# Head of a decoder layer on one core: low parts moved from GpSimd to VectorE, value projections ahead of the compression, block additions in single steps

## The chip, the cores and the metric

The kernel runs on one core of one Trainium2 chip. The metric is device time in microseconds (us) of one execution. Engines are named as in the profile: PE (TensorE matmul), PEld (its weight load), DVE (VectorE), ACT (ScalarE), POOL (GpSimd), SP (SyncE, which here issues the weight loads).

## The reference, cut to what matters

One decoder layer over 512 positions of width 1024, all in float32. What the change touches is the part in front of the attention:

```python
n = rmsnorm(h, g_mix[l])
proj = n @ w_in[l]
(b_gate, c_gate, h_conv, q, k_c, v_c, k_s, v_s, k_w, v_w, g_br, ...) = jnp.split(proj, ...)
k_cmp = compress(kvh(k_c), cmp_pos_k[l], cmp_w1_k[l], cmp_w2_k[l], n_cmp)
v_cmp = compress(kvh(v_c), cmp_pos_v[l], cmp_w1_v[l], cmp_w2_v[l], n_cmp)
o_all = nsa_attention(q, k_cmp, v_cmp, selb(k_s), selb(v_s), winp(k_w), winp(v_w), ...)

def compress(kv, pos, w1, w2, n_cmp):
    blk = kv[:, idx] + pos[None, None, :, None, :]      # 31 blocks of 32 positions, step 16
    return jax.nn.gelu(blk @ w1) @ w2
```

Attention with 16 heads over 4 key and value heads follows (compressed, selected and window branch), then a gated merge with a short convolution, an output projection and a SwiGLU feed-forward block with two RMS norms.

## The kernel before, in words

Every product is made from three matmuls (`mm`, lines 117 to 121): each float32 operand is split into a high part in the matmul type (fp32r) and a low part, the rest, and high by high, high by low and low by high are added in PSUM. So each weight chunk costs, besides its load, one ACT copy that makes the high part `wh` (line 95) and one subtraction that makes the low part `wl` (line 96). `split` (lines 92 to 103) takes the engine of the subtraction as an argument; without one it is GpSimd. The pool `wp` has three buffers each of `raw`, `wh` and `wl`: the load of a chunk waits until the split of the third chunk before it is done, and `wh` waits until PE has used up the third chunk before it.

The order of PE's instructions is the order of the program; the order on the other engines is set by a scheduler at build time, from the program's order, priorities and its own estimate of times. [...]

The head, in the order of PE before the change:

- Lines 187 to 202: eight chunks `wc` (512 columns) with the loads of x. Per chunk ACT makes `nH` and `wh`, DVE makes `nL` (line 192), POOL makes `wl` (DVE for the first chunk alone), PE runs 12 matmuls into four PSUM banks `pc`. This is the projection from which the compressed keys and values are made.
- Lines 210 to 232: `rstd` (its power on POOL, line 211), four small transposes on PE, their copy `rstdb`, and four multiplications that evacuate `pc` into `kcs`, on DVE.
- Line 430, `build_blocks(0)` (lines 235 to 255): eight DVE additions of 64x496 (line 247) and then one ACT copy and one DVE subtraction over 128x2048, which make `bh` and `bl`, the operands of the key compression. `blk`, `bh` and `bl` have one buffer each.
- Line 431: two key projections (`wk`, 1024 columns, 24 matmuls each), evacuated by `k_post` (lines 395 to 412): one DVE multiplication, four ACT copies into `KH`, two DVE subtractions (line 410) and two DVE copies (line 411) into `KL`.
- Lines 432 to 434: four times a quarter of the first value projection (`v_proj(0, q)`, `wv`, 560 columns, 24 matmuls, low part on POOL) followed by a quarter of the key compression (`hidden(0, bk, q)`, `w1`, 1024 columns, 12 matmuls, low part on POOL). The last quarter of `v_proj` is followed by its evacuation (lines 336 to 346, ACT and DVE in turn, eight small instructions each).
- Line 435, `build_blocks(1)`; line 437, `gelu` of the key compression at a raised priority; line 438, the first query projection (`wq`, low part on DVE); lines 439 to 446 the second value projection (low parts on DVE) in turn with the value compression (low parts on POOL), with the transposes of gelu and the small product `k_cmp` between; line 448 the second `gelu`; line 449 one more key projection (`wk[1]`, low part on DVE).
- From line 713 on: attention. `score(0, 0)` (line 476) is its first matmul; the remaining projections are fed between its steps by `Fill`, and their low parts stay on POOL. `gelu_T(gv)` needs the second gelu and stands behind `score(0, 0)`, four steps of the query projection `wq[1]` and `score(0, 1)`.

Of the kernel before, what the change touches and what calls it, by code (L numbers as in the profile page):

```python
# [9 lines left out]
AF = mybir.ActivationFunctionType  # L10
ALU = mybir.AluOpType
# [20 lines left out]
def f(ap):  # L32
    return ap.bitcast(F32)
# [18 lines left out]
def trace(tc, a):  # L52
    nc = tc.nc
# [38 lines left out]
    def split(raw, n, eng=None):  # L92
        h = wp.tile([P, 1024], F32R, name="wh")
        l = wp.tile([P, 1024], F32R, name="wl")
        nc.scalar.activation(h[:, :n], raw[:, :n], AF.Copy)  # L95
        ins = (eng or nc.gpsimd).tensor_tensor(l[:, :n], raw[:, :n], f(h[:, :n]),  # L96
                                               op=ALU.subtract)
        if eng is None and scaled:

            tc.add_manual_dep(ins.ins if hasattr(ins, "ins") else ins, scaled[-1],  # L100
                              mybir.DependencyInfo(mybir.DependencyClass.Sync,
                                                   mybir.DependencyReason.SCHED_ONLY))
        return h, l

    def wchunk(src, n=1024, eng=None):
        return split(load(src, n), n, eng)
# [80 lines left out]
    for k in range(KD):  # L187
        xT = ep.tile([P, S], F32, name="xT", bufs=4)
        nc.sync.dma_start(xT, a["xT"][k])
        raw = load(a["wc"][k], 512)  # L190
        nc.scalar.activation(nH[:, k], xT, AF.Copy, scale=gmix[:, k:k + 1])
        nc.vector.scalar_tensor_tensor(nL[:, k], in0=xT, scalar=gmix[:, k:k + 1],
                                       in1=f(nH[:, k]), op0=ALU.mult, op1=ALU.subtract)
        wh, wl = split(raw, 512, nc.vector if k == 0 else None)
        for m in range(4):
            c = slice(m * P, (m + 1) * P)
            mm(pc[m], (wh[:, c], wl[:, c]), (nH[:, k], nL[:, k]), k == 0, k == KD - 1)
        if 3 <= k < 3 + NT:
            t = k - 3
            xt = ep.tile([P, D], F32, name="xt", bufs=2)  # L200
            nc.sync.dma_start(xt, a["x"][t])
            nc.scalar.activation(xt, xt, AF.Square, accum_out=ss[:, t:t + 1])
# [29 lines left out]
    kcs = kcs[1:] + kcs[:1]  # L232


    def build_blocks(v):
        blk = ep.tile([P, L2, KVH, NB], F32, name="blk")
        nc.gpsimd.memset(blk[:, :, :, NB - 1:NB], 0.0)
        for ct in range(2):
            kc = kcs[2 * v + ct]
            for hp in range(2):  # L240
                rows = slice(hp * HD, (hp + 1) * HD)
                for lp in range(2):
                    s0 = kc[rows, lp:lp + 1]
                    src = bass.AP(tensor=s0.tensor, offset=s0.offset,
                                  ap=[s0.ap[0], [2, L2], [16, NB - 1]])
                    pos = posd[v][rows, lp, :].unsqueeze(2).to_broadcast([HD, L2, NB - 1])
                    nc.vector.tensor_tensor(  # L247
                        blk[lp * HD:(lp + 1) * HD, :, 2 * ct + hp, 0:NB - 1],
                        src, pos, op=ALU.add)
        bh = ep.tile([P, L2, KVH * NB], F32R, name="bh")  # L250
        bl = ep.tile([P, L2, KVH * NB], F32R, name="bl")
        bv = blk.rearrange("p l h n -> p l (h n)")
        nc.scalar.activation(bh, bv, AF.Copy)
        nc.vector.tensor_tensor(bl, bv, f(bh), op=ALU.subtract)
        return bh, bl

    hid = {}

    def hidden(v, b, q):
        if q == 0:  # L260
            hid[v] = tp_tile()[:, 0:256]
        wh, wl = wchunk(a["w1"][v, q])
        for l in range(4):
            l2 = 4 * q + l
            c = slice(l * 256, (l + 1) * 256)
            mm(hid[v], (b[0][:, l2], b[1][:, l2]), (wh[:, c], wl[:, c]), l2 == 0, l2 == L2 - 1)
# [23 lines left out]
    def k_cmp(gT, w):  # L290
        ps = tp_tile()
        o = ps[:, 0:P]
        for c in range(2):
            cc = slice(c * P, (c + 1) * P)
            mm(o, (w[0][:, cc], w[1][:, cc]), (gT[0][:, cc], gT[1][:, cc]), c == 0, c == 1)
        ov = o.rearrange("p (g n) -> p g n", n=NB)
        for ct in range(2):
            oc = ov[:, 2 * ct:2 * ct + 2]
            nc.scalar.activation(KH[ct][:, :, 0:NB], oc, AF.Copy, scale=0.5)
            nc.vector.scalar_tensor_tensor(KL[ct][:, :, 0:NB], in0=oc, scalar=0.5,  # L300
                                           in1=f(KH[ct][:, :, 0:NB]), op0=ALU.mult,
                                           op1=ALU.subtract)
# [18 lines left out]
    def v_proj(br, kh):  # L321
        if kh == 0:
            sct, avt = sc_tile(), av_tile()
            vps[br] = [sct[:, 0:280], sct[:, S:S + 280], sct[:, 2 * S:2 * S + 280], avt[:, 0:280]]
        ps = vps[br]
        wh, wl = wchunk(a["wv"][br, kh], 560, nc.vector if br else None)
        for t in range(NT):
            for kk in range(2):
                k = 2 * kh + kk
                c = slice(kk * 280, (kk + 1) * 280)  # L330
                ts_ = slice(t * P, (t + 1) * P)
                mm(ps[t], (nH[:, k, ts_], nL[:, k, ts_]), (wh[:, c], wl[:, c]),
                   k == 0, k == KD - 1)
        if kh < 3:
            return
        for t in range(NT):
            src = ps[t][:, 0:256].rearrange("p (g d) -> p g d", d=HD)
            r = rstd[:, t:t + 1]
            nc.scalar.activation(VT[:, t, br, :, 0:HD], src, AF.Copy, scale=r)
            nc.vector.scalar_tensor_tensor(VT[:, t, br, :, HD:P], in0=src, scalar=r,  # L340
                                           in1=f(VT[:, t, br, :, 0:HD]), op0=ALU.mult,
                                           op1=ALU.subtract)
            gt = gates[:, t, br * 24:(br + 1) * 24]

            nc.scalar.activation(gt, ps[t][:, 256:280], AF.Exp, scale=nrs[:, t:t + 1])
            nc.vector.tensor_scalar_add(gt, gt, 1.0)
# [48 lines left out]
    def k_post(br, ct):  # L395
        def post(ps):
            kf = oyp.tile([P, S], F32, name="z")
            nc.vector.tensor_tensor(kf, ps, rstdb, op=ALU.mult)
            for hp in range(2):
                me = slice(hp * HD, (hp + 1) * HD)  # L400
                ot = slice((1 - hp) * HD, (2 - hp) * HD)

                def dst(t, rows):
                    return t[ct][rows, hp, NB:KC].rearrange("p (j b c) -> p b j c",
                                                            b=2, c=P)[:, br]

                src = kf[me].rearrange("p (j c) -> p j c", c=P)
                nc.scalar.activation(dst(KH, me), src, AF.Copy)
                nc.scalar.activation(dst(KH, ot), src, AF.Copy)
                nc.vector.tensor_tensor(dst(KL, me), src, f(dst(KH, me)), op=ALU.subtract)  # L410
                nc.vector.tensor_copy(dst(KL, ot), f(dst(KL, me)))
        return post
# [3 lines left out]
    def q_post(pr):  # L416
        def post(ps):
            q = oyp.tile([P, 2, S], F32R, name="q", bufs=2)
            lo, hi = slice(0, HD), slice(HD, P)
            nc.scalar.activation(q[lo, 0], ps[lo], AF.Copy)  # L420
            nc.scalar.activation(q[hi, 1], ps[hi], AF.Copy)
            nc.vector.tensor_tensor(q[hi, 0], ps[lo], f(q[lo, 0]), op=ALU.subtract)
            nc.vector.tensor_tensor(q[lo, 1], ps[hi], f(q[hi, 1]), op=ALU.subtract)
            Q[pr] = q
        return post

    def run(*jobs):
        Fill(jobs).finish()

    bk = build_blocks(0)  # L430
    run(Job(a["wk"][0], k_post(0, 0)), Job(a["wk"][2], k_post(1, 0)))
    for q in range(4):
        v_proj(0, q)
        hidden(0, bk, q)
    bv = build_blocks(1)
    with tc.high_priority(PRI2):
        gk = gelu(hid[0])
    run(Job(a["wq"][0], q_post(0), eng=nc.vector))
    v_proj(1, 0)
    gkT = gelu_T(gk)  # L440
    hidden(1, bv, 0)
    for q in range(1, 4):
        v_proj(1, q)
        if q == 1:
            k_cmp(gkT, w2k)
        hidden(1, bv, q)
    with tc.high_priority(PRI2):
        gv = gelu(hid[1])
    run(Job(a["wk"][1], k_post(0, 1), eng=nc.vector))


    units = [(pr, i) for pr in range(8) for i in range(NT)]
# [604 lines left out]
```

## Time and profile before

| what | us |
|---|---|
| runs of the kernel | 924.97, 927.70, 2294.02; median 927.7 |
| the profiled execution | 930.89 |
| its span, first to last instruction | 929.1 |
| PE busy | 905.9 |
| DVE busy | 521.7 |
| ACT busy | 425.9 |
| POOL busy | 161.3 |
| mean granted TensorE clock, of full | 0.987 |

[...]

### The profile page before, as it was taken

To read this page: it belongs to the slowest core of one execution; us is meant where nothing else is said; L and a number is where in the kernel's file an instruction comes from. 1 tells how busy PE (TensorE), PEld (TensorE's weight loads), DVE (VectorE), ACT (ScalarE), POOL (GpSimd) and SP (SyncE) were. 2 spreads that over 40 slices of the span, in tenths; PEclk is the share of its full clock that TensorE was granted. 3 is DMA by queue.
4 is the path that set the end of the run, shared out by engine and by line. 5 is a ranking of instruction groups with operands and counts; after the bars stand their busy time and mean duration, and the time that the engine had idled before them with its cause. 6 is when DMAs were issued, how large, how long until landed. Compare 5 with 4: busy or idle time off the path is not lost.

```text
span 929.1 us, 12775 instructions
## 1 busy us (share of the span) xinstructions
PE 905.9 (98%) x4757; PEld 766.4 (82%) x4757; DVE 521.7 (56%) x1194; ACT 425.9 (46%) x934; POOL 161.3 (17%) x100
## 2 busy tenths in 40 slices
PE   9878999999999999999999999999999999999996
PEld 7677888888888888878888999888888888888885
DVE  3698688888888788774555552333333333222223
ACT  6254676767667677673433532322332232212222
POOL 5543433232332322222000300000000000000200
PEclk9888999999999999999999999999999999999999
DMA  8323521211212121212622620223323332333212
GB/s 300 103 88 107 170 69 46 69 46 51 64 46 69 46 69 46 69 46 79 239 91 91 202 72 1 91 91 103 102 91 93 109 94 90 92 96 103 96 46 91
DMA packets 26271, 85.15 MB, mean 92 GB/s; under 512 B 3424, under 2 KB 3680, under 8 KB 26208
## 3 DMA queue, kind: packets, MB, share of 16 engines
q1 hardware_dynamic: 24912, 82.78, 27.9%
q10 hardware_dynamic: 1296, 1.55, 0.6%
q8 instruction: 37, 0.61, 0.3%
q14 instruction: 26, 0.21, 0.1%
HBM read 82.23 MB, written 2.10 MB: 91 GB/s over the span
## 4 chain that ended last, share of the span: by engine, by line
PE 89%; DVE 6%; DMA 2%; ACT 1%; issue 1%; POOL 1%; SPq 0%; POOLq 0%; ACTq 0%
PE acc L121 24%; PE acc L119 24%; PE acc L120 24%; PE sc L476 4%; PE tp L543 4%; PE av L561 2%; PE av L562 2%; DVE blk L247 2%; PE av L556 1%; DMA w2kr<-w2k 1%; DVE KL L410 1%; PE sc L120 1%; DMA xt<-x 0%; DMA xT<-xT 0%; PE sc L121 0%
## 5 line engine op out<-in xcount | busy, mean ns | idle before, releaser
L95 ACT ACTIVATE wh<-raw 128x1024 fp32r<-128x1024 f32 (+2 forms) x143 | 144.4, 1012 | 324.2 <-PE acc L120 123.5
L119 PE MATMUL acc<-nH,wh 128*128 128x512 f32 x656 | 263.7, 402 | 0.0
L121 PE MATMUL acc<-nH,wl 128*128 128x512 f32 x656 | 257.7, 393 | 3.4 <-DVE wl L96 3.4
L120 PE MATMUL acc<-nL,wh 128*128 128x512 f32 x656 | 257.2, 392 | 0.0
L96 DVE TENSOR_TENSOR wl<-raw,wh 128x1024 fp32r<-128x1024 f32 (+2 forms) x86 | 106.2, 1235 | 165.7 <-ACT wh L95 165.3
L96 POOL TENSOR_TENSOR wl<-raw,wh 128x1024 fp32r<-128x1024 f32 (+2 forms) x57 | 128.3, 2255 | 241.9 <-DVE pt L519 96.0
L121 PEld LDWEIGHTS acc<-nH,wl 128*128 128x128 f32 x656 | 123.9, 189 | 30.3 <-DVE wl L96 3.9
L120 PEld LDWEIGHTS acc<-nL,wh 128*128 128x128 f32 x656 | 124.3, 189 | 21.8
L119 PEld LDWEIGHTS acc<-nH,wh 128*128 128x128 f32 x656 | 124.3, 189 | 21.7
L121 PE MATMUL acc<-wh,aL 128*128 128x512 f32 (+1 forms) x198 | 73.4, 371 | 0.0
L119 PE MATMUL acc<-wh,aH 128*128 128x512 f32 (+1 forms) x198 | 73.4, 371 | 0.0
L120 PE MATMUL acc<-wl,aH 128*128 128x512 f32 (+1 forms) x198 | 73.4, 370 | 0.0
L503 ACT ACTIVATE pt<-pt,nm 128x128 f32<-128x128 f32 (+3 forms) x128 | 70.7, 554 | 2.4 <-DVE nm L488 1.8
L488 DVE CUSTOM_DVE_ANT_0 pt<-sc,tri,nrs 128x128 f32<-128x128 f32 (+3 forms) x128 | 65.4, 546 | 0.1
L547 DVE TENSOR_TENSOR tl<-tp,th 128x512 fp32r<-128x512 f32 x80 | 55.2, 690 | 13.0 <-ACT th L546 11.2
L894 DVE TENSOR_TENSOR sg<-acc,sg 128x512 f32<-128x512 f32 x22 | 15.2, 692 | 80.7 <-PE acc L121 80.7
L940 POOL TENSOR_TENSOR h<-h,gfin 128x512 f32<-128x512 f32 x4 | 6.0, 1546 | 299.1 <-ACT jk L922 299.1
L546 ACT ACTIVATE th<-tp 128x512 fp32r<-128x512 f32 x80 | 47.4, 593 | 13.0 <-PE tp L543 12.1
L543 PE MATMUL tp<-ident,pt 128*128 128x128 f32 x320 | 49.7, 277 | 0.1
L120 PEld LDWEIGHTS acc<-wl,aH 128*128 128x128 f32 x198 | 37.3, 188 | 7.1
L119 PEld LDWEIGHTS acc<-wh,aH 128*128 128x128 f32 x198 | 37.3, 188 | 7.1
L121 PEld LDWEIGHTS acc<-wh,aL 128*128 128x128 f32 x198 | 37.3, 188 | 7.0
(229 smaller groups left out, 1527.8 us busy)
## 6 DMA issues: line engine op xcount, KB each, us to landing
raw<-wg SPq DMA_DIRECT2D x22, 512.0 KB, 3.5
raw<-wu SPq DMA_DIRECT2D x22, 512.0 KB, 3.5
raw<-wd SPq DMA_DIRECT2D x22, 512.0 KB, 3.5
raw<-wcv SPq DMA_DIRECT2D x12, 512.0 KB, 3.5
raw<-w SPq DMA_DIRECT2D x8, 512.0 KB, 3.5
raw<-wq SPq DMA_DIRECT2D x8, 512.0 KB, 3.5
raw<-wgc SPq DMA_DIRECT2D x8, 512.0 KB, 3.5
raw<-wga SPq DMA_DIRECT2D x8, 512.0 KB, 3.5
```

What stands on the lines that cost most here:

```text
L95: nc.scalar.activation(h[:, :n], raw[:, :n], AF.Copy)
L96: ins = (eng or nc.gpsimd).tensor_tensor(l[:, :n], raw[:, :n], f(h[:, :n]), op=ALU.subtract)
L119: nc.tensor.matmul(ps, lhs[0], rhs[0], start=first, stop=False)
L120: nc.tensor.matmul(ps, lhs[0], rhs[1], start=False, stop=False)
L121: nc.tensor.matmul(ps, lhs[1], rhs[0], start=False, stop=last)
L247: nc.vector.tensor_tensor(blk[lp * HD:(lp + 1) * HD, :, 2 * ct + hp, 0:NB - 1], src, pos, op=ALU.add)
L476: nc.tensor.matmul(o, q[:, h, qs], kk[g // 2][:, g % 2, c0:c0 + n], start=(j == 0), stop=(j == 1))
L488: nc.vector.tensor_tensor_reduce(out=pt[:, r0:r0 + w].rearrange("p (j c) -> p j c", c=P), in0=sv[:, b], in1=tri[:, NT - 1 - i:NT], scale=n ...
L503: nc.scalar.activation(s, s, AF.Exp, scale=-1.0, bias=nm[:, b:b + 1], accum_out=U[u]["sm"][:, h, b:b + 1])
L543: nc.tensor.transpose(tp[:, (2 * b + h) * P:(2 * b + h + 1) * P], pts[h][:, r0:r0 + P], ident)
L546: nc.scalar.activation(th, tp, AF.Copy)
L547: nc.vector.tensor_tensor(tl, tp, f(th), op=ALU.subtract)
```

## The change

`split` of all eight `wc` chunks goes to DVE, and so do those of `w1` (in `hidden`), of both `wv`, of `wk[0]` and `wk[2]`; GpSimd makes no low part before attention starts. `build_blocks` becomes a generator that is stepped by hand (`build(n)`): each of its eight additions is one step, and the ACT copy and DVE subtraction are cut into two halves of 128x1024, one step each. In PE's order both value projections now stand ahead of all of the compression: `wk[0]`, `wk[2]`, the first value projection, `wq[0]`, the second value projection, four quarters of `hidden(0)`, `wk[1]`, four quarters of `hidden(1)` with `k_cmp` in their middle. `wk[1]` no longer stands between the last quarter of `hidden(1)` and `score(0, 0)`. The number of matmuls, loads and splits is as before.

```diff
--- before.py
+++ after.py
@@ -191,7 +191,7 @@
         nc.scalar.activation(nH[:, k], xT, AF.Copy, scale=gmix[:, k:k + 1])
         nc.vector.scalar_tensor_tensor(nL[:, k], in0=xT, scalar=gmix[:, k:k + 1],
                                        in1=f(nH[:, k]), op0=ALU.mult, op1=ALU.subtract)
-        wh, wl = split(raw, 512, nc.vector if k == 0 else None)
+        wh, wl = split(raw, 512, nc.vector)
         for m in range(4):
             c = slice(m * P, (m + 1) * P)
             mm(pc[m], (wh[:, c], wl[:, c]), (nH[:, k], nL[:, k]), k == 0, k == KD - 1)
@@ -231,6 +231,8 @@
         kcs.append(kc)
     kcs = kcs[1:] + kcs[:1]
 
+
+    blocks = {}
 
     def build_blocks(v):
         blk = ep.tile([P, L2, KVH, NB], F32, name="blk")
@@ -247,19 +249,22 @@
                     nc.vector.tensor_tensor(
                         blk[lp * HD:(lp + 1) * HD, :, 2 * ct + hp, 0:NB - 1],
                         src, pos, op=ALU.add)
+                    yield
         bh = ep.tile([P, L2, KVH * NB], F32R, name="bh")
         bl = ep.tile([P, L2, KVH * NB], F32R, name="bl")
         bv = blk.rearrange("p l h n -> p l (h n)")
-        nc.scalar.activation(bh, bv, AF.Copy)
-        nc.vector.tensor_tensor(bl, bv, f(bh), op=ALU.subtract)
-        return bh, bl
+        for c in (slice(0, 8), slice(8, 16)):
+            nc.scalar.activation(bh[:, c], bv[:, c], AF.Copy)
+            nc.vector.tensor_tensor(bl[:, c], bv[:, c], f(bh[:, c]), op=ALU.subtract)
+            yield
+        blocks[v] = bh, bl
 
     hid = {}
 
     def hidden(v, b, q):
         if q == 0:
             hid[v] = tp_tile()[:, 0:256]
-        wh, wl = wchunk(a["w1"][v, q])
+        wh, wl = wchunk(a["w1"][v, q], eng=nc.vector)
         for l in range(4):
             l2 = 4 * q + l
             c = slice(l * 256, (l + 1) * 256)
@@ -323,7 +328,7 @@
             sct, avt = sc_tile(), av_tile()
             vps[br] = [sct[:, 0:280], sct[:, S:S + 280], sct[:, 2 * S:2 * S + 280], avt[:, 0:280]]
         ps = vps[br]
-        wh, wl = wchunk(a["wv"][br, kh], 560, nc.vector if br else None)
+        wh, wl = wchunk(a["wv"][br, kh], 560, nc.vector)
         for t in range(NT):
             for kk in range(2):
                 k = 2 * kh + kk
@@ -427,26 +432,42 @@
     def run(*jobs):
         Fill(jobs).finish()
 
-    bk = build_blocks(0)
-    run(Job(a["wk"][0], k_post(0, 0)), Job(a["wk"][2], k_post(1, 0)))
+
+    V = nc.vector
+
+    def build(n):
+        for _ in range(n):
+            next(bg, None)
+
+    bg = build_blocks(0)
+    run(Job(a["wk"][0], k_post(0, 0), eng=V))
+    build(3)
+    run(Job(a["wk"][2], k_post(1, 0), eng=V))
+    build(3)
+    v_proj(0, 0)
+    build(2)
+    for q in range(1, 4):
+        v_proj(0, q)
+        build(1)
+    bg = build_blocks(1)
+    run(Job(a["wq"][0], q_post(0), eng=V))
     for q in range(4):
-        v_proj(0, q)
-        hidden(0, bk, q)
-    bv = build_blocks(1)
+        v_proj(1, q)
+        build(2)
+    for q in range(4):
+        hidden(0, blocks[0], q)
     with tc.high_priority(PRI2):
         gk = gelu(hid[0])
-    run(Job(a["wq"][0], q_post(0), eng=nc.vector))
-    v_proj(1, 0)
+    build(3)
+    run(Job(a["wk"][1], k_post(0, 1), eng=V))
     gkT = gelu_T(gk)
-    hidden(1, bv, 0)
-    for q in range(1, 4):
-        v_proj(1, q)
-        if q == 1:
-            k_cmp(gkT, w2k)
-        hidden(1, bv, q)
+    hidden(1, blocks[1], 0)
+    hidden(1, blocks[1], 1)
+    k_cmp(gkT, w2k)
+    hidden(1, blocks[1], 2)
+    hidden(1, blocks[1], 3)
     with tc.high_priority(PRI2):
         gv = gelu(hid[1])
-    run(Job(a["wk"][1], k_post(0, 1), eng=nc.vector))
 
 
     units = [(pr, i) for pr in range(8) for i in range(NT)]
```

## Rows read from the trace of the kernel before

**Rows 1.** The page's first part: busy time, share of the span, instructions.
```profile
PE 905.9 (98%) x4757; PEld 766.4 (82%) x4757; DVE 521.7 (56%) x1194; ACT 425.9 (46%) x934; POOL 161.3 (17%) x100
```

**Rows 2.** Waits of PE before 112 us: us in total, times, longest.
```profile
PE sc L120 <- DVE nL L192: 3.5, 1, 3.5
PE acc L121 <- DVE wl L96: 3.4, 1, 3.4
...
PE tp L121 <- DVE bl L254: 1.8, 1, 1.8
PE sc L476 <- ACT gates L345: 1.4, 1, 1.4
PE tp L119 <- ACT bh L253: 1.3, 1, 1.3
PE sc L120 <- POOL wl L96: 1.2, 1, 1.2
```

**Rows 3.** Windows: PE, PEld, DVE, ACT, POOL busy; granted clock, DMA share, GB/s.
```profile
29.40:35.00 5.60, 5.56 (x15) 4.40 (x16) 0.00 (x0) 0.67 (x1) 2.31 (x2) 0.50 0.47 145
...
53.00:59.00 6.00, 6.00 (x26) 5.85 (x27) 5.88 (x6) 1.64 (x4) 4.30 (x3) 0.51 0.30 92
...
76.90:82.90 6.00, 6.00 (x14) 4.75 (x15) 4.79 (x11) 5.41 (x11) 0.17 (x1) 0.51 0.44 135
...
110.70:118.00 7.30, 7.30 (x39) 6.35 (x40) 6.16 (x27) 6.13 (x19) 0.00 (x0) 1.00 0.22 67
30.00:110.70 80.70, 70.88 (x407) 63.48 (x405) 63.20 (x66) 34.10 (x56) 33.95 (x16) 0.88 0.37 117
...
200.00:400.00 200.00, 199.96 (x1118) 166.32 (x1117) 166.03 (x569) 141.92 (x405) 56.49 (x28) 1.00 0.18 56
```

**Rows 4.** DVE by tile: count, shortest/median/longest ns, first and last start.
```profile
L247 DVE TENSOR_TENSOR blk<-xT,posk x8: 994/1012/3004, 38.4 to 47.6; 64x496 f32<-64x496 f32 x8
...
L410 DVE TENSOR_TENSOR KL<-z,KH x6: 679/686/2765, 52.8 to 113.5; 64x512 fp32r<-64x512 f32 x6
L411 DVE CAST KL<-KL x6: 421/1471/2487, 54.2 to 114.6; 64x512 fp32r<-64x512 f32 x6
...
L346 DVE TENSOR_SCALAR gates<-gates x8: 161/175/2362, 77.6 to 110.8; 128x24 f32<-128x24 f32 x8
```

**Rows 5.** Timeline of DVE (first three) and POOL: start us, duration us, instruction.
```profile
20.73 0.75 DVE L192 SCALAR_TENSOR_TENSOR nL<-xT,gmix,nH 128x512 fp32r<-128x512 f32 x1 [2.33 <-ACT nH L191]
...
25.28 1.24 DVE L217 TENSOR_SCALAR nrs<-rstd 128x4 f32<-128x4 f32 x1 [1.14 <-POOL rstd L211]
...
26.51 2.88 DVE L192 SCALAR_TENSOR_TENSOR nL<-xT,gmix,nH 128x512 fp32r<-128x512 f32 x1
...
25.22 6.40 POOL L96 TENSOR_TENSOR wl<-raw,wh 128x512 fp32r<-128x512 f32 x3
```

**Rows 6.** PE timeline: first matmuls of v_proj(1, 3), hidden(1, 3), wk[1]; last of wk[1].
```profile
99.18 0.29 PE L119 MATMUL sc<-wh,nH 128*128 128x280 f32 x1
...
102.30 0.28 PE L119 MATMUL tp<-wh,bh 128*128 128x256 f32 x1
...
103.67 0.40 PE L119 MATMUL acc<-nH,wh 128*128 128x512 f32 x1
...
108.91 0.39 PE L121 MATMUL acc<-nH,wl 128*128 128x512 f32 x1
```

**Rows 7.** Timeline of DVE: two low parts.
```profile
75.59 1.23 DVE L96 TENSOR_TENSOR wl<-raw,wh 128x1024 fp32r<-128x1024 f32 x1
...
85.77 0.73 DVE L96 TENSOR_TENSOR wl<-raw,wh 128x560 fp32r<-128x560 f32 x1
```

**Rows 8.** DVE groups by form before 112 us: count, busy us, mean ns, idle.
```profile
L411 DVE CAST KL<-KL 64x512 fp32r<-64x512 f32 x4 | 7.9, 1978 | 0.1
...
L346 DVE TENSOR_SCALAR gates<-gates 128x24 f32<-128x24 f32 x8 | 5.4, 679 | 0.0
```

**Rows 9.** DMA issues before 112 us: KB each, median us from issue to landing.
```profile
raw<-w SPq DMA_DIRECT2D x8, 512.0 KB, 3.5
```

## Prediction, made before the changed kernel was built or run

> **What bounds the kernel now.** I read the page first: PE has work in flight for 905.9 of 929.1 us [rows 1], so only two things can be won without touching the matmuls: the time in which PE waits, and the time in which it runs at half its clock. The list of PE's waits then puts nearly all of the waiting into the head: six waits before 112 us, 12.6 us together [rows 2]. The reader is to see who ends them: four end with a DVE or POOL instruction, and the other two with an ACT instruction that stands behind DVE in the code (`bh` copies what the additions write, the gates come after `VT`). [...] Head and clock together lose 21.4 us, 2.3% of the kernel. Attention behind it has none to give: 199.96 of 200 us are busy between 200 and 400 us [rows 3].
>
> Why DVE is late is seen in its instructions. The same form takes 1.01 or 3.00 us (block additions), 0.42 or up to 2.49 (copies into `KL`), 0.16 or up to 2.36 (128x24 for the gates) [rows 4]. In the timeline the long ones lie under POOL's low parts: three of these occupy POOL for 6.40 us from 25.22, and in that time the product over 128x4 (line 217) takes 1.24 us and `nL` 2.88, where the `nL` before it took 0.75 [rows 5]. That `nL` ends at 29.39, and PE's wait of 3.5 us ends with it.
>
> **The change part by part.** The matmuls are the same, so PE's own time stays, and the sum is one of waits and clock, made against the profiled execution (930.9 us, span 929.1), which is 3.2 above the median of the runs shown, 927.7.
>
> *Removed, the waits.* If nothing replaced them, `score(0, 0)` would start at 110.7 - 21.4 = 89.3 us. A check from PE's own pace: a value quarter takes 3.12 us, a compression quarter 1.37, a key or query projection 5.47 (5.24 to its last matmul and that one's 0.23) [rows 6]. From the end of `wc`, four projections, eight value quarters, eight compression quarters and 0.8 us (estimate) of small products are 21.9 + 25.0 + 11.0 + 0.8 = 58.7 us.
>
> *The front.* Seven low parts of 512 columns go to DVE, each about 0.7 us by `nL` of the same width (0.75) [rows 5]. With eight `nL` they make 11 us of DVE work in a front of 20, so six are free. For the last chunk I keep the order of the queue (the two small products, which wait for the power on POOL, ahead of `nL`). With POOL free, the first takes about 0.17 instead of 1.24 (as the shortest of the gates [rows 4]), the second likewise, so `nL` runs from 25.6 to 26.3 and its low part to 27.0. PE wanted them at 25.9 (29.4 less its wait) and 0.2 later: a wait of 1.0 us in two pieces, instead of 3.5. Bounds: 0 if the queue puts `nL` first, 3.5 if nothing gets shorter. The low parts of `wk[0]` and `wk[2]`, 1.23 each [rows 7], follow until 29.5, where DVE had nothing to do (0.00 busy from 29.4 to 35.0 [rows 3]). PE finishes `wc` and the transposes at 25.9 + 1.0 + 2.9 = 29.8.
>
> *DVE between there and attention.* Now it is busy 63.2 us from 30.0 to 110.7 [rows 3]. Added: eight low parts of `w1` at 1.23 and four of `wv` at 0.73 [rows 7], 12.8 us. Removed: the lengthening, (1978 - 421) ns x 4 for the copies into `KL`, (679 - 161) ns x 8 for the gates, 2.0 us for one block addition [rows 4, 8], 12.3 us. So DVE has at most 63.7 us of work where PE has 58.7; other forms were longer too (one of line 410 took 2.77 instead of 0.68 [rows 4]), and I put the work at 58. **DVE is then as full as PE**, and its order decides how much waiting is left. Cutting `bh` and `bl` in halves adds nothing that counts.
>
> *First value projection.* All eight additions of the first `blk` and the evacuation of `wk[0]` stand ahead of its third low part. From 29.8: five evacuations of 512 columns at 0.7, eight additions at 1.01, `k_post` (0.7 + 2 x 0.68 + 2 x 0.42), two low parts at 0.73, half a `bl` at 1.2 and the low part itself sum to 17.9 us, so it ends at 47.7; with the second `k_post` ahead of it at 50.6. PE gets there after two projections and two quarters, at 47.0, and wants it 0.2 later. The wait is 0.5 to 3.4 us; I take 1.7, a little under the middle. After that DVE has the time of `wq[0]` and the second value projection, 18 us, for 8 additions, 7 low parts and the evacuation of the first `VT`, about 16, so it catches up. Both `wv` evacuations free the PSUM banks under `wq[0]` or under the compression; the 1.4 us for `gates` at `score(0, 0)` goes.
>
> *Compression in one piece.* From the end of `v_proj(1, 3)` to `score(0, 0)` PE needs 17.2 us (eight quarters, `wk[1]`, the small products). In this time DVE has seven low parts and two halves of `bl` at 1.23, 11.1 us, and some 4 of evacuation, gelu and `k_cmp` (estimate from their widths), none of which can begin earlier, since each low part waits for a buffer that PE frees three chunks before. I take 2.5 us of waits, between 0 (the work fits) and 5 (two low parts late by the 2.2 us of the evacuation). SP's queue: each quarter now needs 512 KB per 1.37 us; a load lands 3.5 us after its issue [rows 9], and the buffer for it is freed about two quarters and more ahead, so loads are hidden; uncovered, they would cost 3.5 - 2 x 1.37 = 0.8 us a quarter. POOL's queue loses the low parts and keeps `rstd`, so the power cannot come later than now.
>
> *Behind it.* The second gelu had 5.47 us of `wk[1]` as its cover; now it has `score(0, 0)`, four steps and `score(0, 1)`, about 3.8 us, for a chain of five instructions on two engines, and the low part of `wq[1]` is still POOL's and can lengthen one of them by 2. I take 1.0, between 0 and 3.
>
> *Clock.* The waits that halved it were 3.4 us or more, or two of 1.3 and 1.8 close together [rows 2, 3]; after the single 1.4 it stayed at 1.00 [rows 3]. One more stretch costs 2.9; I take 0.8, for a chance of about 0.3; bounds 0 and 5.8.
>
> Sum of what comes back: 1.0 + 1.7 + 2.5 + 1.0 + 0.8 = 7.0, so 14.4 us are saved; the check by PE's pace (29.8 + 58.7 + 1.7 + 2.5 + 0.8 = 93.5 instead of 110.7, less 1.0) gives 16.2. I take 15.5: 930.9 - 15.5 = 915.4, and less 3.2 for the median **912 us**. All bounds at the low end save 21.4 us by the waits and 23.2 by PE's pace (906 and 905), all at the high end 0.9 us (927).
>
> **The rivals.** *A, the queue fits.* Waits vanish but for the front: 20.4 us, 907. For it: the additions are single steps and DVE had idle time. Against: 58 us of work in 58.7.
>
> *B, one or two low parts come late by the length of a few additions*, as `wl` did before 76.9 us: each is 3.4 of wait and 2.9 of clock, 6.3; with one more than forecast 918, with two 925. For it: the order was laid out at build time on estimates, and DVE has no slack to mend it.
>
> *C, slower.* The long DVE instructions are not POOL's doing, or go to other waits, and DVE's queue sets the pace of the head: 12.8 us are added between 30 and 110.7 and nothing goes, 927.7 + 12.8 = 940.5. It decides from where less than 12.8 us of lengthening goes away and DVE's idle time stays. Against: the long ones begin and end with POOL's [rows 5].
>
> *D, many small waits hold the clock down.* Three more half-clock stretches of 2.9 us, 921. Against: 1.00 after the wait of 1.4 [rows 3]. [...]
>
> **How the numbers follow.** The forecast has 0.56, A 0.16, B 0.18, C 0.05, D 0.05. About 2% (18.6 us, to 909.1) is what a measurement of this kernel can tell from no change. Faster by more: all of A and a third of the forecast, 0.34. Slower by more (946): under half of C, 0.02. The rest, 0.64, is within. The range leaves out part of B, C and the lowest of A: 905 to 922; the forecast's own is 907 to 917.
>
> **What would show it.** In the profile after, `score(0, 0)` should start at 93 to 96 us; DVE's copies into `KL` at 0.42 and additions at 1.0; no wait of PE over 3 us; one wait for `nL` or `wl` of `wc` near 1 us; waits of 1 to 3 us on `wl` at the second or third value quarter and in the compression; POOL nearly idle from 26 us until `wq[1]`. The step on DVE's load is wrong if DVE is under 85% busy from 30 us to `score(0, 0)`; the whole is wrong if PE's waits there exceed 10 us, or if new waits appear in attention.

## The result and the profile after

The kernel after the change takes 919.18 us (median of 5 runs, 917.53 to 920.69), the kernel before in the same measurement 926.2 (median of four runs, 924.97 to 927.70). One more run of the kernel before, 2294.02 us, was disturbed and is left out here, while the 927.7 from which the forecast starts is a median that counts it. The ratio is 0.9922 with a 95% interval of 0.9899 to 0.9944: faster by some 7 us, inside the forecast range, but less than half of the 15.7 us that were forecast.

The profiled execution after is the fastest of its five, 917.53 us with a span of 915.7. The page's first part, after, against [rows 1]:

```profile
PE 898.8 (98%) x4757; PEld 760.2 (83%) x4757; DVE 515.5 (56%) x1217; ACT 426.3 (47%) x936; POOL 119.6 (13%) x79
```

PE's instructions are the same and its busy time is 7.1 us less: that is clock (8.8 us were lost to it before, half of the 17.6 us that [rows 3] show at 0.50 and 0.51; 1.7 are below). POOL lost 21 low parts and 41.7 us, DVE took them and is 6.2 us *less* busy. What PE waits for before 112 us, after (us in total, times, longest), against [rows 2]:

```profile
PE sc L119 <- ACT gates L350: 2.6, 1, 2.6
PE sc L120 <- DVE wl L96: 2.5, 1, 2.5
PE tp L184 <- DVE bh L181: 1.9, 1, 1.9
PE tp L120 <- DVE wl L96: 1.6, 2, 1.1
PE tp L119 <- ACT wh L95: 0.2, 1, 0.2
```

The third of these stands at the very start and is in every kernel here; the others make 6.9 us where there were 13.3 (the 12.6 of [rows 2], and 0.7 for one `wh` that the prediction's six waits leave out). No wait in the front is long enough for this list, but two matmuls of the last chunk start 0.52 and 0.60 us behind the one before them, where the pace is 0.23. So some 0.7 us are lost there in two pieces. PE's timeline after:

```profile
24.47 0.39 PE L119 MATMUL sc<-nH,wh 128*128 128x512 f32 x1
24.99 0.50 PE L120 MATMUL sc<-nL,wh 128*128 128x512 f32 x1
25.59 0.50 PE L121 MATMUL sc<-nH,wl 128*128 128x512 f32 x1
```

The windows after (columns as in [rows 3]):

```profile
29.40:35.00 5.60, 5.60 (x26) 4.65 (x25) 5.54 (x9) 0.67 (x1) 0.00 (x0) 1.00 0.38 102
...
45.20:50.00 4.80, 4.74 (x25) 4.74 (x26) 4.67 (x8) 3.81 (x6) 0.00 (x0) 0.64 0.35 109
...
64.30:70.00 5.70, 5.70 (x44) 5.70 (x45) 3.16 (x6) 2.23 (x4) 0.00 (x0) 1.00 0.39 126
...
30.00:97.20 67.20, 60.25 (x386) 54.99 (x386) 56.06 (x82) 34.91 (x58) 1.91 (x2) 0.97 0.39 120
200.00:400.00 200.00, 199.96 (x1123) 166.72 (x1123) 163.30 (x560) 140.23 (x398) 55.58 (x26) 1.00 0.17 54
```

One stretch of lowered clock is left, 0.64 over 4.8 us, which costs 0.36 x 4.8 = 1.7 us; there were three of some 6 us. Attention is as before. `score(0, 0)` starts at 97.21 instead of 110.70, 13.5 us earlier, and what follows it takes as long as before (818.5 and 818.4 us to the end of the span). So the whole difference between these two executions is in the head.

DVE by tile after (columns as in [rows 4]):

```profile
L249 DVE TENSOR_TENSOR blk<-xT,posk x8: 981/1010/1027, 32.9 to 42.9; 64x496 f32<-64x496 f32 x8
L249 DVE TENSOR_TENSOR blk<-xT,posv x8: 989/1010/1029, 51.0 to 62.3; 64x496 f32<-64x496 f32 x8
...
L415 DVE TENSOR_TENSOR KL<-z,KH x8: 674/685/690, 38.7 to 116.1; 64x512 fp32r<-64x512 f32 x8
L416 DVE CAST KL<-KL x8: 410/421/423, 40.3 to 117.0; 64x512 fp32r<-64x512 f32 x8
...
L351 DVE TENSOR_SCALAR gates<-gates x8: 166/168/177, 61.0 to 81.8; 128x24 f32<-128x24 f32 x8
```

The reader is to see the third number of each: the longest is now within 6% of the median, where it had been 3 to 15 times the shortest. In these groups the lengthening is gone.

Two waits remain that count. PE's timeline after:

```profile
45.26 0.40 PE L120 MATMUL sc<-wl,nH 128*128 128x280 f32 x1 [2.53 <-DVE wl L96]
...
61.30 0.39 PE L121 MATMUL acc<-nH,wl 128*128 128x512 f32 x1
64.28 0.39 PE L119 MATMUL sc<-wh,nH 128*128 128x280 f32 x1 [2.59 <-ACT gates L350]
```

The first is the second quarter of the first value projection. The second is the first matmul of the second value projection: it writes into the PSUM banks of the first, and waits until these are evacuated. DVE's timeline there, after:

```profile
57.00 2.03 DVE L249 TENSOR_TENSOR blk<-xT,posv 64x496 f32<-64x496 f32 x2
59.06 0.49 DVE L345 SCALAR_TENSOR_TENSOR VT<-sc,rstd,VT 128x256 fp32r<-128x256 f32 x1
59.58 1.01 DVE L249 TENSOR_TENSOR blk<-xT,posv 64x496 f32<-64x496 f32 x1
60.62 0.48 DVE L345 SCALAR_TENSOR_TENSOR VT<-av,rstd,VT 128x256 fp32r<-128x256 f32 x1
...
62.33 0.99 DVE L249 TENSOR_TENSOR blk<-xT,posv 64x496 f32<-64x496 f32 x1
63.35 0.18 DVE L351 TENSOR_SCALAR gates<-gates 128x24 f32<-128x24 f32 x1
63.43 0.48 DVE L345 SCALAR_TENSOR_TENSOR VT<-sc,rstd,VT 128x256 fp32r<-128x256 f32 x1
```

Additions of the *second* block (`posv`), which nobody needs until the value compression, stand ahead of and between the four `VT` that free the banks (the third `VT` is among the lines left out).

### The profile page after: what moved, and what is told of

Read it like the earlier page. It is cut to its first block, busy times and chain, and to the rows that moved or that the text cites. A ratio compares the mean times of both kernels' runs of the same rounds, so it can differ in the third digit from the quotient of the medians.

```text
span 915.7 us, 12776 instructions
## 1 busy us (share of the span) xinstructions
PE 898.8 (98%) x4757; PEld 760.2 (83%) x4757; DVE 515.5 (56%) x1217; ACT 426.3 (47%) x936; POOL 119.6 (13%) x79
## 4 chain that ended last, share of the span: by engine, by line
PE 88%; DVE 6%; DMA 2%; ACT 2%; issue 1%; SPq 0%; POOL 0%; POOLq 0%; ACTq 0%; DVEq 0%
PE acc L119 24%; PE acc L121 24%; PE acc L120 24%; PE sc L497 4%; PE tp L564 4%; PE av L582 2%; PE av L583 2%; DVE blk L249 2%; DVE wl L96 1%; PE av L577 1%; DMA w2kr<-w2k 1%; DMA raw<-wk 1%; ACT wh L95 1%; DMA xT<-xT 0%; DMA xt<-x 0%
## 5 line engine op out<-in xcount | busy, mean ns | idle before, releaser
L96 DVE TENSOR_TENSOR wl<-raw,wh 128x1024 fp32r<-128x1024 f32 (+2 forms) x107 | 123.4, 1154 | 170.1 <-ACT wh L95 170.0
L119 PEld LDWEIGHTS acc<-nH,wh 128*128 128x128 f32 x656 | 123.4, 188 | 21.4
L96 POOL TENSOR_TENSOR wl<-raw,wh 128x1024 fp32r<-128x1024 f32 x36 | 86.6, 2407 | 236.7 <-DVE pt L540 96.4
```

Source lines behind the costliest of these rows:

```text
L119: nc.tensor.matmul(ps, lhs[0], rhs[0], start=first, stop=False)
```

## The experiments

Ten runs follow: the two kernels once more, unchanged, and eight kernels with edits. Each computes all that the kernel before does; one adds work whose result nobody reads.

**Was the profiled execution of before a usual one?** The two kernels, unchanged, were profiled once more.

> The kernel before, unchanged, once more. Theory P (the profiled execution of before that the prediction was read from lost more in the head than its usual execution): this execution takes 924 to 928 us instead of 930.9, score(0, 0) starts 3 to 6 us earlier than at 110.7, with a granted clock above 0.987 because one of the three half-clock stretches is gone or short. Rival Q (the head is always the same, and the 4 to 5 us by which the profiled execution stood above the others lie behind it): score(0, 0) starts between 110 and 111.4 us again whatever the time, and the stretch behind it is shorter than 818.4 us.

> The changed kernel, unchanged, once more. Theory P: the waits are the same ones (2.5 for a low part of the first value projection, 2.6 for the gates, 1.8 in the compression), score(0, 0) starts between 97 and 100 us, and what the time is above 917.5 us is found in the head as half-clock time. Rival Q: score(0, 0) starts at 97.2 again and the rest is behind it.

The kernel before took 922.83 us this time, with `score(0, 0)` at 101.98, 8.7 us earlier than in the execution of [rows 2, 3], which is more than theory P had said. What follows takes 819.1 us, much as before, so rival Q falls. PE's timeline of this second execution:

```profile
26.12 0.50 PE L120 MATMUL sc<-nL,wh 128*128 128x512 f32 x1 [0.34 <-DVE nL L192]
...
44.66 0.39 PE L119 MATMUL tp<-wh,bh 128*128 128x256 f32 x1 [1.31 <-ACT bh L253]
46.99 0.39 PE L121 MATMUL tp<-wh,bl 128*128 128x256 f32 x1 [1.83 <-DVE bl L254]
49.53 0.60 PE L120 MATMUL sc<-wl,nH 128*128 128x280 f32 x1 [0.94 <-POOL wl L96]
57.95 0.40 PE L120 MATMUL sc<-wl,nH 128*128 128x280 f32 x1 [1.15 <-POOL wl L96]
...
101.98 0.30 PE L476 MATMUL sc<-KH,q 128*128 128x288 f32 x1
```

The wait for `nL` is 0.34 instead of 3.54, and the one for `gates` is gone. DVE's timeline in the front shows how, against [rows 5]:

```profile
24.08 1.26 DVE L217 TENSOR_SCALAR nrs<-rstd 128x4 f32<-128x4 f32 x1 [1.14 <-POOL rstd L211]
...
25.32 0.73 DVE L192 SCALAR_TENSOR_TENSOR nL<-xT,gmix,nH 128x512 fp32r<-128x512 f32 x1
```

The same `nL` takes 0.73 instead of 2.88. POOL works on low parts at that time in both executions; what differs is which of the two instructions starts first. POOL's low part of `wk[0]`, in the first and in the second execution:

```profile
26.49 2.35 POOL L96 TENSOR_TENSOR wl<-raw,wh 128x1024 fp32r<-128x1024 f32 x1
```

```profile
25.40 2.91 POOL L96 TENSOR_TENSOR wl<-raw,wh 128x1024 fp32r<-128x1024 f32 x1
```

In the first, POOL's instruction starts 0.02 us before `nL` (26.51 [rows 5]), and `nL` is the long one. In the second, `nL` starts 0.08 us before POOL's instruction, and POOL's is longer by 0.56 us. The kernel with the order alone (below) repeats the first case; POOL's timeline and DVE's there:

```profile
25.33 2.34 POOL L96 TENSOR_TENSOR wl<-raw,wh 128x1024 fp32r<-128x1024 f32 x1
```

```profile
25.36 2.86 DVE L192 SCALAR_TENSOR_TENSOR nL<-xT,gmix,nH 128x512 fp32r<-128x512 f32 x1
```

In the first execution of before the last quarter of x also landed later: the square that reads it (line 202) starts at 22.79 us, in the second at 21.59. But with the order alone it starts at 21.62, and `nL` is long all the same. So a late x is not needed for this loss: in these three executions it goes with which instruction starts first, and there a few hundredths of a microsecond lie between the two.

Identified losses in this execution: waits 0.3 + 1.3 + 1.8 + 2.1 + 3.4 = 8.9 us and about 5 of clock (0.50 from 50 to 55 us, 0.84 and 0.72 in two more stretches of 5), 14 instead of 21.4 (22.1 with the 0.7 for `wh`). The 46 runs of the kernel before beside the experiments lay between 920.73 and 930.62 us, with medians of 926.53, 925.36 and 925.95: the execution I had argued from (930.89) was slower than all of them, the second one among the fastest. The kernel after took 920.08 in its second execution, `score(0, 0)` at 99.42, with the waits in the same places (2.4 and 0.8 for `wl`, 3.0 for `gates`, 1.6 in the compression). So a single profile lay 4 to 5 us off the median for the kernel before, and 1 to 2 us for the kernel after.

**Which part carries the gain?** First the low parts alone, in the order of before, and then the new order with the low parts left on POOL. The edits of the first, all four of the kind

```diff
-        wh, wl = wchunk(a["w1"][v, q])
+        wh, wl = wchunk(a["w1"][v, q], eng=nc.vector)
```

(`wc`, `w1`, first `wv`, `wk[0]` and `wk[2]`); the second undoes them in the kernel after.

> Before, with the head's low parts on DVE and nothing else changed (order, blocks in one piece). Theory (POOL's share of the loss: front wait of 3.5 and its clock, lengthened DVE instructions): the front wait goes (3.5 + 2.8 us), copies into KL fall to 0.42; the waits on bh and bl stay because the eight additions still stand in one block, 12.8 us of new DVE work stands between 30 us and attention. I expect 4 to 7 us faster than before (920 to 923). Rival (DVE is the bound as soon as it makes the low parts, whatever the order): 0 to 4 us slower.

> The changed kernel, with the low parts of the head back on GpSimd as before (wc from the second chunk, w1, wk[0], wk[2], first wv). Theory: the order takes away the waits on bh, bl and the second projection's wl, but DVE instructions are lengthened again and the front wait of 3.5 with its half-clock stretch comes back: 0 to 4 us faster than before (923 to 927), 4 us or more slower than the changed kernel. Rival (the order carries the gain): within 2 us of the changed kernel (917 to 921).

Low parts alone: 919.51, ratio 0.9929 (0.9909 to 0.995), as much as the whole change, and 7.0 us by the medians, the most that the theory had said. Order alone: 927.26, ratio 1.001 (0.999 to 1.003), nothing, where the theory had 0 to 4 us. With the order alone PE's largest waits were for POOL (4.4 us in five pieces in the compression, 2.0 in the value projection), 2.6 for `nL` and 2.4 for a low part on DVE. In its profile (930.01, the slowest of its runs) `score(0, 0)` starts at 104.32, between the two executions of before, but what follows takes 823.9 us, where it takes 818.4 to 819.1 in the four profiles above. There PE waits 1.68 and 1.65 us for DVE's `KL` and `nm` right behind `score(0, 0)`, which is where the prediction feared for the second gelu.

So the whole measured gain is that of the engine of the low parts; the new order neither adds nor costs what can be told. How the gain divides between low parts that PE itself awaits from POOL (2.1 us in the second execution of before) and DVE instructions that POOL lengthens was not measured.

**How much of it is the front?** The low parts of `wc` alone, and all the others without those of `wc`:

```diff
-        wh, wl = split(raw, 512, nc.vector if k == 0 else None)
+        wh, wl = split(raw, 512, nc.vector)
```

> The kernel before with one edit: the low parts of the seven later wc chunks go to DVE; everything behind the front as before. Theory (the front's wait of 3.5 us and the half clock behind it belong to the one profiled execution, another look at the kernel before had 0.3 us there): ratio 0.998 to 1.000, no more than 2 us won, PE's waits behind the front as before (wl L96 about 3.4, POOL wl 2, bl and bh 3). Rival (the front wait is usual, 3.5 + 2.8 us as in the first profile): 5 to 6 us won, ratio 0.994.

> The kernel before with all the other low parts of the change on DVE (w1, the first wv, wk[0], wk[2]) and those of wc still on POOL. Theory: the gain sits here, ratio 0.993 to 0.995 (5 to 7 us won, most of what low parts alone gave), with the DVE copies into KL at 0.42 and waits left for bl and wl of some 5 us. Rival (half or more of the gain is the front's): ratio 0.997 or above.

Front alone: 923.84 against 925.95, ratio 0.9967 (0.9952 to 0.9983), 2.1 us by the medians and 1.6 to 4.4 by the interval. All but the front: 920.3, ratio 0.9941 (0.9911 to 0.9971), 5.7 us. The theory had said at most 2, the rival 5 to 6: the front's usual worth lies at the edge of the theory or above it, and below the rival. The lowest runs with and without this edit are alike (921.33 and 922.00 us), the highest are not (925.00 and 929.58), as fits a loss that only some executions have.

The two gains add up to 7.8, low parts alone gave 7.0, and the two kernels don't part the change cleanly. In the second one the low part of `wk[0]`, which is what `nL` met in the first execution of before, is on DVE, so that the loss of the front can't come in that way; PE's wait for `nL` was 0.58 us in its profile.

**Does POOL's work lengthen DVE's?** The kernel after with 28 subtractions on POOL whose result nobody reads, from 30 us on:

```diff
+    scr = ep.tile([P, S], F32, name="scr")
+    for _ in range(28):
+        nc.gpsimd.tensor_tensor(scr, rstdb, rstdb, op=ALU.subtract)
```

> The changed kernel, with 28 subtractions over 128x512 added on GpSimd behind rstdb, which nothing waits for; they take GpSimd some 36 us, from about 30 us on. Theory L (GpSimd's work by itself lengthens DVE's instructions): copies into KL and block additions show times of 1.5 us or more again, PE's waits grow by several us, 5 to 15 us slower than the changed kernel. Rival (in the kernel before, DVE and PE waited only for GpSimd's results): DVE's durations stay at 0.42 and 1.01, within 1.5 us of the changed kernel.

937.36 us in its single run, 18 more than after and more than the 5 to 15 of theory L. POOL is busy with the 28 from 30.3 to 73.7 us. DVE by tile, this kernel (columns as above):

```profile
L253 DVE TENSOR_TENSOR blk<-xT,posk x8: 1018/1636/1736, 32.7 to 49.6; 64x496 f32<-64x496 f32 x8
...
L420 DVE CAST KL<-KL x8: 421/784/1215, 44.1 to 136.5; 64x512 fp32r<-64x512 f32 x8
```

and PE's waits before 115 us, this kernel:

```profile
PE sc L120 <- DVE wl L96: 12.8, 2, 10.0
PE sc L119 <- ACT gates L354: 6.5, 1, 6.5
```

The instructions that the change had made short are long again, though DVE's 1217 instructions stand in the same order as in the kernel after. The two waits left after the change grow from 5.1 to 19.3 us (the one for `wl` in two pieces). That POOL's work lengthens DVE's instructions even where nobody needs its result (medians of 1.64 us instead of 1.01 for the first block's additions, 0.78 instead of 0.42 for the copies), and that the lengthening reaches PE, is thereby shown.

**What do the two waits left cost, and do they trade?** One edit holds the second block's additions on DVE behind the first value evacuation, by a dependency that the scheduler alone sees (`nm` takes the instruction out of its wrapper); one gives the value chunks' low parts a raised priority; a third does both.

```diff
-                    nc.vector.tensor_tensor(
+                    ins = nc.vector.tensor_tensor(
...
+                    if v == 1:
+                        tc.add_manual_dep(nm(ins), nm(evac[0]).name, mybir.DependencyInfo(
+                            mybir.DependencyClass.NoSync, mybir.DependencyReason.SCHED_ONLY))
...
-            nc.vector.tensor_scalar_add(gt, gt, 1.0)
+            evac[br] = nc.vector.tensor_scalar_add(gt, gt, 1.0)
```

```diff
-        wh, wl = wchunk(a["wv"][br, kh], 560, nc.vector)
+        with tc.high_priority(PRI2):
+            wh, wl = wchunk(a["wv"][br, kh], 560, nc.vector)
```

> The changed kernel, with the eight additions of the second block held back in DVE's queue until the first value projection is evacuated. Theory W (the 2.6 to 3.0 us wait for the PSUM banks at v_proj(1, 0) comes from additions that stand ahead of the evacuation in DVE's queue): that wait goes, score(0, 0) starts 2 to 3 us earlier, 2 to 3.5 us faster than the changed kernel (916 to 917). Rival (the evacuation is limited by its own chain of ACT and DVE, or the held additions come late for the compression): the wait stays above 1.5 us or a new one of the same size appears, within 1 us of the changed kernel.

> The changed kernel, with the value projections' chunks at a raised priority, so that their low parts stand ahead of most block additions. Theory W: the wait of 2.4 to 2.5 us in the first value projection goes, and with it the half-clock stretch that follows it in some executions; 2 to 4 us faster than the changed kernel (915 to 917). Rival (DVE's total work is the limit, so the wait only moves): another wait of DVE's grows by as much, within 1 us.

> Both edits together. Theory W: both waits go, score(0, 0) starts at 91 to 93 us, 912 to 915 us, which is what the prediction had for the changed kernel; only the waits in the compression (1.6 to 1.8) are left. Rival (DVE is full): the two add up to no more than one of them, 916 to 919.

Held additions: 916.79, ratio to before 0.9912 (0.9881 to 0.9943), the `gates` wait gone and `score(0, 0)` at 95.59. That is theory W's time; but this kernel and the kernel after were not measured side by side. Their medians differ by 2.4 us, their ratios to before by 0.001 (0.9 us), and the intervals overlap, so what the removed wait is worth is not shown. Low parts first: 921.95, ratio 0.9965 (0.9948 to 0.9983), slower than the kernel after, which neither theory W nor the rival had said. Its wait for `wl` is down to 0.33, and PE is done with `wq[0]` 2.3 us earlier (at 59.4 us instead of 61.7); but the evacuation ends 0.6 us later, and the other wait grows. PE's timeline:

```profile
64.88 0.60 PE L119 MATMUL sc<-wh,nH 128*128 128x280 f32 x1 [5.49 <-ACT gates L351]
```

So here 2.2 us of wait removed at one place came back as 2.9 at the next, and the granted clock was 0.57 in the 5 us from 65 us. Both together: 913.75, ratio 0.9887 (0.9854 to 0.9921), `score(0, 0)` at 91.48, clock 0.999, as theory W had said. PE's waits before `score(0, 0)` in that kernel:

```profile
PE tp L184 <- DVE bh L181: 1.9, 1, 1.9
PE tp L120 <- DVE wl L96: 1.6, 2, 1.1
PE acc L121 <- DVE wl L96: 0.3, 1, 0.3
PE tp L119 <- ACT wh L95: 0.2, 1, 0.2
```

This is the best kernel of the study, 5.4 us under the kernel after by the medians and 3.2 by the ratios. They were not measured side by side, but its slowest run (915.56) is faster than the fastest of the kernel after (917.53). Behind `score(0, 0)` it takes 820.2 us, 1.7 more than the kernel after, with a new wait of 0.90 us for `nm`. Whether the held additions would do the same in the old order was not tried.

## Why the prediction was wrong

The mechanism held: POOL's low parts lengthened DVE's instructions (copies into `KL` took up to 2.49 us), without them the lengthening went (0.42 at most), DVE's queue set the waits that remained, and nothing changed behind the head. The size was off by 7.2 us (919.18 against 912), in three steps. The 21.4 us that the forecast starts from are the six waits, 12.6 [rows 2], and half of the 17.6 us at 0.50 and 0.51, 8.8 [rows 3], or 2.9 a stretch.

**The largest: "against the profiled execution (930.9 us), which is 3.2 above the median", subtracted on both sides at the end.** That takes the 3.2 for something that both kernels have. It lay in the very terms that were to be removed: a wait for `nL` of 3.5 us with 2.8 of clock behind it, and 1.4 for `gates`, of which a second execution had 0.3, none, and none. The front was to give 2.5 of wait and 2.8 of clock; alone it gave 2.1 by the medians, and in the executions above its loss came only where POOL's instruction started ahead of `nL`. Nor was 3.2 the excess: against the 926.2 above it was 4.7, and how that divides among the waits is open. Profile against profile the change saved 930.89 - 917.53 = 13.4 us, 2.1 less than the 15.5 forecast. The other 5.1 are that the profile after lies 1.65 *under* its median where mine was to lie 3.2 above (together 4.9; the rest is rounding).

**"Both `wv` evacuations free the PSUM banks under `wq[0]`", at nothing.** The cover was there, but the evacuation's DVE steps stood in the queue behind and among the second block's additions: 2.6 and 3.0 us in two profiles. I had named these additions as work for that time, and not asked where in the queue they stood. Holding them back removed the wait (2.4 us by the medians, not clear of noise).

**The first value projection: 1.7 us.** It measured 2.5 in one profile, with 1.7 of clock behind it, and 2.4 + 0.8 in the other, and mainly at the second quarter instead of the third: one low part stood behind the additions and the second key's product. The place was out by a quarter, the size within the bounds (0.5 to 3.4).

The other terms erred the other way: the front 0.7 instead of 1.0 (in two pieces, as forecast), the compression 1.8 instead of 2.5, the second gelu none of the 1.0 (PE is busy 7.79 of 7.80 us behind `score(0, 0)`). What came back in the listed waits and the clock sums to 6.9 + 1.7 = 8.6 us in the profile, against 7.0, so this half of the sum was 1.6 short, or 2.3 with the front. The first execution of before had lost 22.1, and 22.1 - 8.6 is the 13.5 us by which `score(0, 0)` moved. Two bounds of the range are also summed wrongly: with all at the low end the waits give 20.9 and PE's pace 22.7 us, since the first value projection starts at 0.5, and with all at the high end 0.7 are saved, not 0.9.

**DVE's load.** I put it at 58 us and asked for 85% busy; it was 56.1 of 67.2, 83%, which by my own sign makes the step wrong. The mean hides the point. The windows after:

```profile
30.00:64.30 34.30, 29.18 (x163) 26.01 (x162) 33.64 (x47) 14.12 (x25) 0.22 (x1) 0.95 0.26 74
64.30:97.20 32.90, 31.07 (x224) 28.98 (x225) 22.42 (x36) 20.78 (x34) 1.69 (x1) 1.00 0.52 167
```

DVE is 98% busy in the first half and 68% in the second, and the eight additions of the second block, some 8 us that only the second half needs, lie in the first (51.0 to 62.3 us in the rows by tile). I had counted work against time over the whole head, where each half has to be counted by itself. Of the other signs, the start of `score(0, 0)` was missed (97.21 and 99.42 us, not 93 to 96); the short copies and additions, no wait over 3 us, and the waits for `wl` came as named.

**The rivals.** *A* (the queue fits) is nearly what held additions and raised low parts together made of the head (`score(0, 0)` at 91.5, where A's 20.4 us less would be 90.3). *B* (low parts late by a few additions) described one of the two waits left, at 2.5 us and not 3.4, and its other victim was the evacuation. That its 918 for one more late low part is close to 919.18 is luck: it priced each at 6.3 us. *C* falls: the lengthening is POOL's (the first block's additions at a median of 1.64 us with the added subtractions, at 1.01 without). *D* falls too: the waits of 0.48, 0.20 and 1.12 us in the compression left the clock at 1.00, as the window after shows, and so did the five waits for POOL, 4.4 us together, in the compression of the order alone (1.00 from 84 to 104 us):

```profile
75.00:97.20 22.20, 20.37 (x143) 18.27 (x142) 17.98 (x29) 16.43 (x28) 1.69 (x1) 1.00 0.57 184
```

With three waits in the one profile and five in the other, this is a weak test of D.

## What to carry to other kernels

Before a wait is counted as removable, look for it in a second execution: a profile that lies above the median has its excess somewhere, and often in just the waits that stand out. When work moves to an engine that becomes nearly full, go through its queue stretch by stretch, and ask of each instruction by when it is needed; here additions without haste stood ahead of an evacuation that PE waited for. And an idle engine isn't always free to use: here POOL's work beside DVE lengthened DVE's instructions (the first block's additions from a median of 1.01 to one of 1.64 us).

## What the runs showed of the hardware

**The price of POOL's company.** With POOL subtracting without pause, DVE's timeline and POOL's:

```profile
39.50 1.64 DVE L253 TENSOR_TENSOR blk<-xT,posk 64x496 f32<-64x496 f32 x1
41.07 1.48 DVE L419 TENSOR_TENSOR KL<-z,KH 64x512 fp32r<-64x512 f32 x1
42.58 1.64 DVE L253 TENSOR_TENSOR blk<-xT,posk 64x496 f32<-64x496 f32 x1
44.15 1.21 DVE L420 CAST KL<-KL 64x512 fp32r<-64x512 f32 x1
45.40 1.42 DVE L419 TENSOR_TENSOR KL<-z,KH 64x512 fp32r<-64x512 f32 x1
```

```profile
38.65 7.62 POOL L237 TENSOR_TENSOR scr<-rstdb 128x512 f32<-128x512 f32 x5
```

From 39.50 to 45.40 DVE does in 5.9 us what takes it 1.01 + 0.69 + 1.01 + 0.42 = 3.1 us alone (medians of the kernel after). POOL takes 7.62 / 5 = 1.52 each, where the shortest of the 28 was 1.04, so in 5.9 us it does 5.9 / 1.52 x 1.04 = 4.0 us of work. The two sum to 7.1 us in 5.9, as if the engines mostly took turns, with about 1.2 us in parallel (an estimate from these rows). In the front the later of the two was the longer one: `nL` at 2.88 and 2.86 us where it started 0.02 and 0.03 us behind POOL's instruction, and POOL's at 2.91 instead of 2.35 where it started 0.08 behind `nL`. But full turns would take 7.1 us here, and 5.9 were measured; in what way the two hinder each other, no run shows.

**The same wait, two clocks.** After waits of 2.53 and 2.59 us in one execution the granted clock was 0.64 in the stretch behind the first and 1.00 behind the second; in another execution of the same kernel it was 1.00 behind 2.39 and 0.76, and 0.66 in the 5 us behind 3.00. I had taken from [rows 2, 3] that it takes 3.4, or two close together. In these runs a wait of 2.4 to 3 us is followed by 1.00 or by a mean of 0.64 to 0.66 over some 5 us, and what decides was not settled.
